# The first feed-forward's down product as seven half-size products, in a hybrid retention and attention block

## Chip, cores and metric

One core of one Trainium2 chip. The time is the device time of one execution in microseconds. A kernel's figure is the median of its runs.

## The reference

One layer on 528 tokens (16 meta tokens and 512 of the input) of width 1024, in float32: a feed-forward, a mixer, a second feed-forward and a last norm.

```python
h = h + 0.5 * swiglu(rmsnorm(h, ffn1_norm), ffn1_w_gate, ffn1_w_up, ffn1_w_down)
h = h + hybrid_mixer(rmsnorm(h, mix_norm), ...)
h = h + 0.5 * swiglu(rmsnorm(h, ffn2_norm), ffn2_w_gate, ffn2_w_up, ffn2_w_down)
y = rmsnorm(h, final_norm)

def swiglu(u, w_gate, w_up, w_down):
    return (jax.nn.silu(u @ w_gate) * (u @ w_up)) @ w_down
```

The hidden width is 2816, that is 22 feature blocks of 128. The change lies in the first line: the product with `ffn1_w_down` ("the downs").

## The kernel before

**Numbers in two parts.** TensorE multiplies in a reduced format (fp32r), so every operand is split into an upper part (a rounded copy by ScalarE) and a lower part (the rest, a subtraction by VectorE; `in_two`, lines 284 and 285). A product then takes three matmuls: upper by upper, upper by lower, lower by upper (`mm3`, line 157). A block of weights is the stationary operand, 264 tokens (half of 528) the moving one.

**The first feed-forward** (class `Sevens`, object `s1`, and the lists of steps from line 868). Feature blocks go in pairs. A pair is two halves, the gate and the up; each half is one `seven` (line 440): a 2 by 2 block product done as seven half-size products instead of eight, in four steps. Run1 has the products X and Z, run2 adds to X and starts Y, run3 adds to X again and then to Y, run4 adds the last product, T4, to X. Between these, ScalarE copies partial sums out of the PSUM banks (`copy`), and VectorE takes results out (`take`, lines 512 and 526). In run3, `take(3)` reads X between the third product and T4. VectorE also makes sums of the weights for the next half (`pre2`, `pre3`, lines 458 to 464). At the end of an up half the product of gate and up lies in a tile `u`; it is split into the hidden tiles `hh` and `hl`.

**The downs before.** `down(f0, nf, taken_by)` (line 831) multiplies the hidden tiles of `nf` feature blocks by their rows of the weights: eight steps, one for each 128 output columns, each with `nf` x 3 x 2 matmuls of 128x264. The two results of a step are added by VectorE with factor 0.5 to the residual `hT` (line 849). There are four groups: blocks 0 to 3 first, then after each three pairs the six blocks these made. In the last of three pairs (`soon`) the hidden tiles are made at once.

**Leaving the stage.** In the last group each finished column tile of `hT` goes through `leave_tokens` (line 861): multiplied by the gain and split (ScalarE `xh`, line 121; VectorE `xl`, line 122), squared by ScalarE and added to the sum of squares by GpSimd (`add_square`, lines 255 and 256), and stored to DRAM on ScalarE's queue. The mixer's first tiles (`early_step`, line 947; 24 matmuls of 128x384 for the first) need these `xh` and `xl`, all eight column tiles; behind the first one TensorE does the norm's small matmuls (`rstd_steps`, line 218), which need the full sum of squares.

**What sets the order.** `steps_through` (line 295) runs all steps of the stage as one list: at step i it issues the loads and preparations of step i+4 (`pre`), the upper split of step i+2, then the matmuls of step i with the lower split of step i+2 among them. TensorE, ScalarE and VectorE keep the order of the program here; DMA queues (SP above all) and GpSimd are ordered by the framework's planner. Work put into the list `behind` is done at the next `catch_up`, after the first step's second product.

**The second feed-forward** has the change's form already (lines 2200 and on): the downs of 16 of its 22 blocks are seven products behind all of its pairs, with operands kept in DRAM (`hx`, `wx`). There GpSimd makes the differences of the hidden tiles (line 2289), and VectorE makes the block sums of the weights during the attention (`block_sums`, line 1908).

## Time and profile before

| | |
|---|---|
| median of 3 runs | 1516.91 us (1515.62 to 1517.08) |
| the profiled execution | 1517.71 us, its span 1515.9 us |
| TensorE busy | 1505.0 us, 99% of the span, 9743 matmuls |
| VectorE busy | 1137.9 us, 75% |
| ScalarE busy | 729.4 us, 48% |
| GpSimd busy | 156.6 us, 10% |
| granted TensorE clock | 0.999 of full speed |
| HBM | 180.06 MB read, 32.78 MB written, 140 GB/s over the span |

In the rows below PE is TensorE, DVE VectorE, ACT ScalarE, POOL GpSimd and SP the engine that issues most DMAs; SPq is its queue. A row of the timeline has the start in us, the duration in us, engine, line, operation and operands (out<-in), the count, and in brackets the idle time in front of it with what ended it. L157 is line 157 of the kernel before.

### The profile page before, as it was taken

How to read it: one execution, taken by the hardware profiler on the slowest of the kernel's cores; microseconds unless marked ns; L12 is line 12 of the kernel's file. 1: busy time of each engine (PE TensorE's matmuls, PEld its weight loads, DVE VectorE, ACT ScalarE, POOL GpSimd, SP SyncE). 2: the span in 40 equal slices, each digit the busy share in tenths (PEclk: the TensorE clock that was granted, in tenths of full speed). 3: DMA queues.
4: the chain of work that ended last, by engine and by line, in shares of the span. 5: the costliest groups of instructions: out<-in, count | busy, mean ns of one | idle time of the engine just before them, and what ended most of it. 6: DMA issues, size and time to landing. Idle time of an engine off the chain costs nothing.

```text
span 1515.9 us, 24279 instructions
## 1 busy us (share of the span) xinstructions
PE 1505.0 (99%) x9743; PEld 1359.7 (90%) x9743; DVE 1137.9 (75%) x1735; ACT 729.4 (48%) x1156; POOL 156.6 (10%) x188
## 2 busy tenths in 40 slices
PE   9999999999999999999999999999999999999997
PEld 8999999999988888788888889989888889999986
DVE  4988585786786767677968676777665779999877
ACT  5655263454354444542323445555335445555565
POOL 1000000003111120000000021111002003322101
PEclk9999999999999999999999999999999999999999
DMA  5132323226544444232222476456573224445792
GB/s 169 58 120 89 114 96 112 85 97 201 202 148 168 167 148 155 87 122 86 94 86 85 111 187 178 155 168 214 173 255 108 84 83 147 152 162 174 248 330 109
DMA packets 170176, 217.03 MB, mean 143 GB/s; under 512 B 7056, under 2 KB 126504, under 8 KB 169168
## 3 DMA queue, kind: packets, MB, share of 16 engines
q1 hardware_dynamic: 156592, 180.97, 36.5%
q0 software_dynamic: 9072, 26.59, 5.9%
q10 hardware_dynamic: 4400, 7.94, 1.5%
q8 instruction: 76, 1.25, 0.3%
q14 instruction: 36, 0.29, 0.1%
HBM read 180.06 MB, written 32.78 MB: 140 GB/s over the span
## 4 chain that ended last, share of the span: by engine, by line
PE 95%; DMA 2%; issue 1%; DVE 1%; ACT 1%; POOL 0%; POOLq 0%; ACTq 0%; DVEq 0%; SPq 0%
PE psqX L157 14%; PE psd L157 8%; PE psqY L157 7%; PE psrg L157 6%; PE psro L157 4%; PE psvX L1150 4%; PE psqZ L157 3%; PE psrk L157 3%; PE psak L157 3%; PE psu L157 3%; PE psrq L157 3%; PE psmo L157 3%; PE psga L157 3%; PE psat L157 3%; PE psaq L157 3%; PE psg L157 2%
## 5 line engine op out<-in xcount | busy, mean ns | idle before, releaser
L285 DVE TENSOR_TENSOR wlo<-raw,whi 128x1024 fp32r<-128x1024 f32 (+2 forms) x193 | 212.6, 1103 | 44.9 <-ACT whi L284 44.9
L284 ACT ACTIVATE whi<-raw 128x1024 fp32r<-128x1024 f32 (+2 forms) x193 | 179.6, 931 | 121.2 <-PE psd L157 37.7
L157 PE MATMUL psqX<-th,whi 128*128 128x264 f32 (+1 forms) x432 | 123.0, 285 | 0.0
L157 PE MATMUL psqX<-tl,whi 128*128 128x264 f32 (+1 forms) x432 | 122.3, 283 | 0.0
L157 PE MATMUL psqX<-th,wlo 128*128 128x264 f32 (+1 forms) x432 | 122.2, 283 | 0.0
L117 ACT ACTIVATE whi<-raw 128x1024 fp32r<-128x1024 f32 (+1 forms) x58 | 60.3, 1043 | 88.5 <-DMA raw<-in_w_in_dram 21.6
L284 ACT ACTIVATE whi<-wsum 128x1024 fp32r<-128x1024 f32 x72 | 76.1, 1057 | 53.6 <-issue 22.9
L118 DVE TENSOR_TENSOR wlo<-raw,whi 128x1024 fp32r<-128x1024 f32 (+1 forms) x58 | 69.8, 1204 | 42.5 <-ACT whi L117 42.2
L285 DVE TENSOR_TENSOR wlo<-wsum,whi 128x1024 fp32r<-128x1024 f32 x72 | 86.9, 1215 | 2.7 <-ACT whi L284 2.7
L157 PEld LDWEIGHTS psqX<-th,whi 128*128 128x128 f32 x432 | 82.0, 190 | 0.5
L157 PEld LDWEIGHTS psqX<-tl,whi 128*128 128x128 f32 x432 | 82.0, 190 | 0.0
L157 PEld LDWEIGHTS psqX<-th,wlo 128*128 128x128 f32 x432 | 82.0, 190 | 0.0
L157 PE MATMUL psro<-vo,whi 128*128 128x512 f32 x256 | 79.3, 391 | 0.0
L157 PE MATMUL psd<-hl,whi 128*128 128x264 f32 x352 | 71.2, 284 | 0.0
L157 PE MATMUL psd<-hh,wlo 128*128 128x264 f32 x352 | 70.9, 283 | 0.0
L157 PE MATMUL psd<-hh,whi 128*128 128x264 f32 x352 | 70.6, 282 | 0.0
L256 POOL TENSOR_TENSOR ssum<-ssum,sq 128x528 f32<-128x528 f32 (+1 forms) x14 | 18.4, 1317 | 396.4 <-ACT sq L255 396.4
L157 PEld LDWEIGHTS psro<-vo,whi 128*128 128x128 f32 x256 | 48.0, 188 | 10.7 <-ACT whi L284 0.2
L157 PEld LDWEIGHTS psd<-hh,wlo 128*128 128x128 f32 x352 | 54.5, 188 | 0.0
L157 PEld LDWEIGHTS psd<-hh,whi 128*128 128x128 f32 x352 | 54.3, 188 | 0.0
L157 PEld LDWEIGHTS psd<-hl,whi 128*128 128x128 f32 x352 | 53.9, 188 | 0.0
L157 PE MATMUL psrg<-xh,whi 128*128 128x512 f32 x128 | 51.8, 405 | 0.0
(478 smaller groups left out, 4645.6 us busy)
## 6 DMA issues: line engine op xcount, KB each, us to landing
raw<-in_ffn_w_up_dram SPq DMA_DIRECT2D x22, 1024.0 KB, 5.0
raw<-in_ffn_w_gate_dram SPq DMA_DIRECT2D x21, 1024.0 KB, 5.6
raw<-in_w_in_dram SPq DMA_DIRECT2D x19, 1024.0 KB, 5.1
raw<-in_w_in_dram SPq DMA_DIRECT2D x31, 512.0 KB, 3.9
w<-in_w_in_dram SPq DMA_DIRECT2D x24, 512.0 KB, 6.3
raw<-in_ffn_w_down_dram SPq DMA_DIRECT2D x22, 512.0 KB, 5.0
raw<-in_ffn_w_down_dram SPq DMA_DIRECT2D x12, 768.0 KB, 4.4
raw<-in_w_ret_out_dram SPq DMA_DIRECT2D x8, 1024.0 KB, 4.8
```

The lines of the kernel that those rows point to most:

```text
L117: nc.scalar.activation(hi, src, AF.Copy)
L118: eng.tensor_tensor(lo, src, hi.bitcast(F32), ALU.subtract)
L157: nc.tensor.matmul(o, a[:, k, :], b[:, sl], start=first and k == 0 and i == 0, stop=last and k == nk - 1 and i == 2, skip_group_check=onto)
L256: eng.tensor_tensor(ssum[:, :n], ssum[:, :n], sq[:, :n], ALU.add)
L284: nc.scalar.activation(hi, src, AF.Copy)
L285: return lambda: nc.vector.tensor_tensor(lo, src, hi.bitcast(F32), ALU.subtract)
L1150: nc.tensor.matmul(d[bank_][t], a, b[:, k, :], start=not onto and j + k + m == 0, stop=j + k == 3 and m == 2, skip_group_check=onto)
```

## The change

The four groups become: `down(0, 4)` as before, then all nine pairs of blocks 4 to 21 in one row, then a unit for the blocks 4 to 19 of seven products X, Z, U, Q, V, Y, W with a `down(20, 2)` in front of W. In a product, each of four steps has 4 x 2 x 3 matmuls of 128x264. Its operands come from DRAM: `hx1` holds the hidden tiles' four quarters and four differences of them (made by VectorE in `spill1`, behind each pair), `wx1` four sums of quarters of the down weights (made by VectorE in `sums1`, two at a time, in `pre3` of 16 sevens; their blocks are loaded by `bring1` and stored again on SP's queue). The hidden tiles of blocks 4 to 19 are no longer split in the pair, but as operands of the unit. Left column tiles (0 to 3) are finished by the last step of W, right ones (4 to 7) by `down(20, 2)`, whose steps run in the order 4, 5, 6, 7, 0, 1, 2, 3. The first early tile multiplies tiles 4 to 7 before 0 to 3. `product1` (shortened below) is the new function of the unit.

```diff
@@ Sevens
+        extra = []
@@ pre3
                 self.sum4 = lambda: nc.vector.tensor_tensor(s[:, 3], raw[:, 4:, c1], s[:, 0], ALU.subtract)
+                if self.extra:
+                    self.extra.pop(0)()
@@ leaving the stage
-        def leave_tokens(k):
-
-            h, l = new_x(k, XO)
-            split_gain(hT[k], gains[:, 1, k : k + 1], h, l)
-            add_square(hT[k], ssum2, k == 0, sqp[0], bufs=4)
-            nc.scalar.dma_start(hd[k], hT[k][:, REAL])
+        def split_tokens(k):
+            split_gain(hT[k], gains[:, 1, k : k + 1], *new_x(k, XO))
+        def leave_tokens(k, eng=nc.gpsimd, queue=nc.scalar):
+            add_square(hT[k], late["s"], k == 4, sqp[0], bufs=4, eng=eng)
+            queue.dma_start(hd[k], hT[k][:, REAL])
...
+        def spill1(f, u):
+            k = (f - F0) // 2
+            all4 = hidp.tile([P, 2, TX], F32, tag=turn(room_tags), name="ts")[:, :, :T].rearrange("p a (b t) -> p a b t", b=2)
+            ts = [all4[:, i // 2, i % 2] for i in range(4)]
+            for t, a, b in zip(ts, (u[:, 1], u[:, 3], u[:, 3], u[:, 2]), (u[:, 0], ts[0], u[:, 1], ts[1])):
+                nc.vector.tensor_tensor(t, a, b, ALU.subtract)
+            nc.gpsimd.dma_start(hx1[0:4, :, k, :].rearrange("o p t -> p o t"), u)
+            for i in range(2):
+                nc.gpsimd.dma_start(hx1[4 + 2 * i : 6 + 2 * i, :, k, :].rearrange("o p t -> p o t"), all4[:, i])
+        def bring1(k):
+            blocks["now"] = []
+            for tag, (half, cs) in zip(("R", "R", "ssum2", "wq"), BLOCKS):
+                t = hidp.tile([P, S], F32, tag="wq", name="wq") if tag == "wq" else one_row(tag)[:, :S]
+                nc.sync.dma_start(t, wrows1[half][:, k, cs])
+                blocks["now"].append(t)
+        def sums1(k, which):
+            ts = blocks["now"]
+            for i in which:
+                to, x, y, op = BLOCK_SUMS[i]
+                nc.vector.tensor_tensor(ts[to], ts[x], ts[y], op)
+                nc.sync.dma_start(wx1[i, :, k, :], ts[to])
+            if 3 in which and k < 7:
+                bring1(k + 1)
+        s1.spill = {f: (lambda u, f=f: s1.behind.append(lambda: spill1(f, u))) for f in range(F0, F1, 2)}
+        s1.extra = [lambda k=k, w=w: sums1(k, w) for k in range(8) for w in ((0, 1), (2, 3))]
+        def product1(tag, src, which, pool_of, taken, onto=None):
...
+                def run(w, lower, j=j, d=d):
+                    if j == 0 and onto is None:
+                        streams[tag] = [unit[pool_of].tile([P, S], F32, tag="bank", name=f"ps{tag}")[:, :TH] for _ in range(4)]
+                    pss = streams[onto or tag]
+                    h, l = (d["xp"][:, i] for i in range(2))
...
+                    for c in range(4):
+                        for k in range(2):
+                            for i, (a, m) in enumerate(((w[0], h), (w[0], l), (w[1], h))):
+                                nc.tensor.matmul(pss[c], a[:, k, c * P : (c + 1) * P], m[:, k, :],
...
+                        if c == 0:
+                            lower()
+                        if last:
+                            taken(c, pss[c])
+                        if c == 1:
+                            s1.catch_up()
+                            if behind:
+                                behind.pop(0)()
+        def right_done(c):
+            if c >= 4:
+                behind.append(lambda: (split_tokens(c), leave_tokens(c)))
+            if c == 1:
+                ahead[0] = 4
+            if c in (1, 3):
+                behind.pop(0)()
+        def left_done(c, ps):
+            added1((1, 0))(c, ps)
+            split_tokens(c)
+            if c == 3:
+                for k in range(4):
+                    leave_tokens(k, nc.vector, nc.sync)
         steps = down(0, 4, keep_sums)
-        groups = (4, 10, 16)
-        for f0 in groups:
-            for f in range(f0, f0 + 6, 2):
-                steps += s1.pair_steps(f, f == f0 + 4)
-            if f0 != groups[-1]:
-                steps += down(f0, 6, keep_sums)
+        for f in range(F0, NF, 2):
+            steps += s1.pair_steps(f, False)
         n_busy = len(steps)
-        steps += down(groups[-1], 6, leave_tokens)
+        steps += product1("X", wrows1[0][:, :, C1], 0, "A", added1((0, 0)))
+        steps += product1("Z", wrows1[1][:, :, C1], 2, "B", added1((0, 0)))
+        steps += product1("U", wx1[2], 5, None, added1((1, 0)), "X")
+        steps += product1("Q", wrows1[1][:, :, C2], 7, "B", added1((0, 1)))
+        steps += product1("V", wx1[1], 6, None, added1((1, 1), (0, 1)), "X")
+        steps += product1("Y", wx1[0], 4, "B", added1((1, 1)))
+        steps += down(F1, 2, right_done, (4, 5, 6, 7, 0, 1, 2, 3), load_row)
+        steps += product1("W", wx1[3], 3, None, left_done, "Y")
@@ early_step
-                mm3(outs, w, xs, KD)
+                if i == 0:
+                    mm3(outs, [t[:, 4:] for t in w], lambda k: xs(k + 4), 4, True, False)
+                    mm3(outs, [t[:, :4] for t in w], xs, 4, False, True)
+                else:
+                    mm3(outs, w, xs, KD)
@@ running the steps
+        bring1(0)
+        pipe = steps_through(steps, ahead)
...
             wss.close()
+            unit["p"] = sqs.enter_context(pool("f1u", 1, side="right"))
             sqp.append(sqs.enter_context(pool("sq", 1, side="right")))
+            ahead[0] = 6
+            bankst.close()
+            for name in "AB":
+                unit[name] = bankst.enter_context(pool(f"f1{name}", 4, PSUM))
+            s1.banks = unit["A"]
```

`ahead` is how many steps ahead the loads are issued: 4 until the unit begins, then 6, and 4 again near its end.

## Rows read from the trace of the kernel before

**Rows 1.** The page: busy times, and the chain that ended last by engine.
```profile
PE 1505.0 (99%) x9743; PEld 1359.7 (90%) x9743; DVE 1137.9 (75%) x1735; ACT 729.4 (48%) x1156; POOL 156.6 (10%) x188
...
PE 95%; DMA 2%; issue 1%; DVE 1%; ACT 1%; POOL 0%; POOLq 0%; ACTq 0%; DVEq 0%; SPq 0%
```

**Rows 2.** The chain in order of time, 60 to 400 us (start, us, what).
```profile
62.28 23.15 PE psd L157 x192
...
146.29 34.56 PE psd L157 x288
...
371.33 4.20 PE psiq L157 x24
```

**Rows 3.** Busy us by engine in the window of one middle pair.
```profile
105.60:125.80 20.20, 20.20 (x170) 20.20 (x170) 17.68 (x25) 12.26 (x19) 0.00 (x0) 1.00 0.27 88
```

**Rows 4.** Timeline of VectorE in that pair: gate half, then up half.
```profile
107.75 1.22 DVE L285 TENSOR_TENSOR wlo<-wsum,whi 128x1024 fp32r<-128x1024 f32 x1
108.89 0.42 DVE L512 TENSOR_TENSOR g<-psqZ,p 128x264 f32<-128x264 f32 x1
109.23 0.68 DVE L458 TENSOR_TENSOR wsum<-raw 128x512 f32<-128x512 f32 x1
109.95 0.69 DVE L459 TENSOR_TENSOR wsum<-wsum,raw 128x512 f32<-128x512 f32 x1
110.55 0.68 DVE L285 TENSOR_TENSOR wlo<-raw,whi 128x512 fp32r<-128x512 f32 x1
111.16 0.69 DVE L463 TENSOR_TENSOR wsum<-raw 128x512 f32<-128x512 f32 x1
113.17 0.43 DVE L512 TENSOR_TENSOR g<-psqX,p 128x264 f32<-128x264 f32 x1 [1.33 <-PE psqX L157]
...
119.29 1.25 DVE L285 TENSOR_TENSOR hl<-g,hh 128x1056 fp32r<-128x1056 f32 x1
120.46 0.68 DVE L458 TENSOR_TENSOR wsum<-raw 128x512 f32<-128x512 f32 x1
```

**Rows 5.** Timeline of VectorE and TensorE at the first pair.
```profile
82.13 0.68 DVE L463 TENSOR_TENSOR wsum<-raw 128x512 f32<-128x512 f32 x1
...
93.50 0.42 DVE L512 TENSOR_TENSOR g<-psqX,p 128x264 f32<-128x264 f32 x1
...
93.98 0.39 PE L157 MATMUL psqX<-th,whi 128*128 128x264 f32 x1
```

**Rows 6.** Timeline of VectorE in a gate half of the second feed-forward.
```profile
1303.58 1.58 DVE L463 TENSOR_TENSOR wsum<-raw 128x512 f32<-128x512 f32 x1
1305.08 0.41 DVE L512 TENSOR_TENSOR g<-psqX,p 128x256 f32<-128x256 f32 x1
```

**Rows 7.** DMA issues (KB, us to landing); a window of the second unit.
```profile
raw<-in_ffn_w_up_dram SPq DMA_DIRECT2D x22, 1024.0 KB, 5.0
...
wq<-in_ffn_w_down_dram SPq DMA_DIRECT2D x32, 256.0 KB, 5.1
...
1440.40:1451.30 10.90, 10.90 (x49) 9.02 (x49) 7.80 (x9) 6.33 (x8) 0.00 (x0) 1.00 1.04 405
```

**Rows 8.** Timeline where the mixer's first tiles begin, by engine.
```profile
371.71 0.76 DVE L849 SCALAR_TENSOR_TENSOR hT<-psd,hT 128x264 f32<-128x264 f32 x2
...
372.50 0.74 ACT L121 ACTIVATE xh<-hT,gains 128x528 fp32r<-128x528 f32 x1 [2.32 <-DVE hT L849]
373.15 0.63 ACT L255 ACTIVATE sq<-hT 128x528 f32<-128x528 f32 x1
...
373.27 0.77 DVE L122 SCALAR_TENSOR_TENSOR xl<-hT,gains,xh 128x528 fp32r<-128x528 f32 x1 [0.80 <-ACT xh L121]
373.92 1.35 POOL L256 TENSOR_TENSOR ssum<-ssum,sq 128x528 f32<-128x528 f32 x1 [3.21 <-ACT sq L255]
374.76 1.60 DVE L285 TENSOR_TENSOR wlo<-raw,whi 128x1024 fp32r<-128x1024 f32 x1 [0.71 <-ACT whi L284]
375.37 1.24 PE L218 MATMUL psn<-ones,ssum 128*128 128x1 f32 x10
```

More of the change, by code (lines that the diff above doesn't have):

```diff
@@ L258 @@
     R = cpool.tile([P, T], F32, name="R", tag="R", bufs=2)
-    R2 = cpool.tile([P, T], F32, name="R2", tag="R", bufs=2)
+    late = {}
     ssum2 = cpool.tile([P, T], F32, name="ssum2", tag="ssum2")
@@ L271 @@
     wx = dpool.tile([4, P, 8, S], F32, name="wx")
+    hx1 = dpool.tile([8, P, 8, TH], F32, name="hx1")
+    wx1 = dpool.tile([4, P, 8, S], F32, name="wx1")
+    F0, F1 = 4, 20
+    C1, C2 = slice(0, S), slice(S, D)
+    wrows1, wrows = (w[F0 * P : F1 * P, :].rearrange("(k two p) c -> two p k c", two=2, p=P) for w in (wd1, wd2))
+    BLOCK_SUMS = ((1, 2, 1, ALU.add), (2, 0, 2, ALU.subtract), (0, 1, 0, ALU.subtract), (3, 3, 0, ALU.subtract))
+    BLOCKS = ((0, C1), (1, C2), (0, C2), (1, C1))
     def gap(p, n):
@@ new lines, in product1, with pre, upper @@
+        def product1(tag, src, which, pool_of, taken, onto=None):
+            steps, ws = [], []
+            for j in range(4):
+                d = {}
+                def pre(j=j, d=d, ws=ws):
+                    is_late = ahead[0] > 4 or "p" in unit
+                    if j % 2 == 0:
+                        t = unit["p"].tile([P, 2048], F32, tag="wr", name="raw", bufs=2) if is_late and j == 0 else \
+                            wpool.tile([P, 2048], F32, tag="raw", name="raw", bufs=2)
+                        ws.append(t.rearrange("p (k c) -> p k c", k=4))
+                    d["w"] = ws[j // 2][:, j % 2 * 2 : j % 2 * 2 + 2]
+                    nc.sync.dma_start(d["w"], src[:, 2 * j : 2 * j + 2, :])
+                    d["x"] = unit["p"].tile([P, T], F32, tag="xr", name="raw", bufs=6) if is_late else one_row(turn(raw_tags))
+                    nc.sync.dma_start(d["x"].rearrange("p (k t) -> p k t", k=2), hx1[which, :, 2 * j : 2 * j + 2, :])
+                def upper(d=d):
+                    hi, lo = (wpool.tile([P, 1024 + WPAD], F32R, tag=t, name=t, bufs=3)[:, w_at[0] :][:, : 2 * S]
+                              .rearrange("p (k c) -> p k c", k=2) for t in ("whi", "wlo"))
+                    lower_w = in_two(d["w"], hi, lo)
+                    xp = hidp.tile([P, 2, TX], F32R, tag=turn(part_tags), name="xp")[:, :, :T]
+                    lower_x = in_two(d["x"], xp[:, 0], xp[:, 1])
+                    d["xp"] = xp.rearrange("p a (k t) -> p a k t", k=2)
+                    return hi, lo, lambda: (lower_w(), lower_x())
+                def run(w, lower, j=j, d=d):
[3 more added lines that the diff above has]
+                    h, l = (d["xp"][:, i] for i in range(2))
+                    first, last = j == 0 and onto is None, j == 3
+                    for c in range(4):
+                        for k in range(2):
+                            for i, (a, m) in enumerate(((w[0], h), (w[0], l), (w[1], h))):
+                                nc.tensor.matmul(pss[c], a[:, k, c * P : (c + 1) * P], m[:, k, :],
+                                                 start=first and k == 0 and i == 0, stop=last and k == 1 and i == 2,
+                                                 skip_group_check=onto is not None)
+                        if c == 0:
[6 more added lines that the diff above has]
+                                behind.pop(0)()
+                steps.append((pre, upper, run))
+            return steps
@@ new lines, in added1, with taken @@
+        def added1(*to):
+            def taken(c, ps):
+                for half, right in to:
+                    h = hT[4 * right + c][:, (one, two)[half]]
+                    nc.vector.scalar_tensor_tensor(h, ps, 0.5, h, ALU.mult, ALU.add)
+            return taken
+        def right_done(c):
[5 more added lines that the diff above has]
+                behind.pop(0)()
@@ L911, in normed_out @@
         def normed_out(i):
-            ps, r = early_ps[i], R2[:, early[i][1]]
+            ps, r = early_ps[i], late["R"][:, early[i][1]]
             if i > 6:
@@ L1241 @@
             wss.close()
+            unit["p"] = sqs.enter_context(pool("f1u", 1, side="right"))
             sqp.append(sqs.enter_context(pool("sq", 1, side="right")))
-            for _ in range(n_dense - n_busy - 4):
+            ahead[0] = 6
[3 more added lines that the diff above has]
+            s1.banks = unit["A"]
+            for _ in range(8):
+                next(pipe)
+            late["R"] = cpool.tile([P, T], F32, name="R2", tag="R", bufs=2)
+            late["s"] = cpool.tile([P, T], F32, name="ssum2", tag="ssum2")
+            for _ in range(n_dense - n_busy - 12):
                 next(pipe)
```

37 lines of the change are left out of this document (22 added, 15 removed).

## The prediction, made before the changed kernel was run

> **What bounds the kernel now.** First the page: TensorE is busy 99% of the span and makes up 95% of the chain that ended last [rows 1], so nothing else is worth asking about until it delays TensorE. Second, the chain in order of time over the first feed-forward and the mixer's first tiles [rows 2]: each down group is one unbroken piece of matmuls, 192 in 23.15 us and 288 in 34.56 us (three such groups), 0.120 us per matmul. A group of the change's kind can therefore only win by issuing fewer matmuls, and only if the other engines follow. Third, then, the engine nearest to its limit: in a middle pair of feature blocks TensorE is busy 20.20 of 20.20 us and VectorE 17.68 [rows 3]. Fourth, VectorE's own order in that pair [rows 4], where the reader should look at starts, not durations: a 0.69 us instruction is followed 0.60 us later.
>
> The profiled execution took 1517.71 us, 0.80 above the median of the three timed runs (1516.91). I sum differences against the profiled one and apply them to the median.
>
> **Matmuls.** 16 feature blocks x 8 column tiles x 2 token halves x 3 parts are 768 matmuls of 128x264. Seven products x 4 steps x 4 column tiles x 2 blocks x 3 parts are 672, of the same shape. They change the stationary block at every matmul, as the pairs do, whose 168 take 20.2 us [rows 3], also 0.120 each. So 96 x 0.120 = **-11.5 us**. ScalarE's and VectorE's splits for the unit (per step of 24 matmuls, 2.88 us: VectorE 1.14 for 1024 columns, 107.75 to 108.89 in rows 4, and about 0.62 for 528) lie beside it.
>
> **Pairs, VectorE.** Gone is the lower half of the hidden tile, 1.17 us from start to start (119.29 to 120.46). New are four token differences of 128x264, 0.34 each by the nearest row (108.89 to 109.23), and four block sums of 128x512, 0.60 each (109.95 to 110.55). An instruction that reads its predecessor's result starts 0.12 later (109.23 to 109.95), once in each four. So 17.68 - 1.17 + 1.48 + 2.52 = 20.5 us in a pair of 20.2: VectorE has nothing left. Where it hurts is run4. Its product T4 adds to the bank that VectorE must first read in run3 (`take(3)`); between them lie 12 matmuls, 1.44 us. In a gate half VectorE now reaches that read 1.33 us early [rows 4]. The differences (1.48) and two block sums (1.20) come ahead of it: 1.35 late, plus the read's 0.43 and 0.06 to TensorE, less 1.44: a stop of 0.4 us. In the up half the two block sums stand in for the hidden tile (1.20 against 1.17) and no stop follows. Pairs 2 to 8 have both in their gate half: 7 x 0.4 = 2.8.
>
> The first pair is worse. There VectorE is already behind from the first down: it reaches the read at 93.50 without any wait, the read ends at 93.92, and T4 starts at 93.98 [rows 5]. Block sums are issued behind the pre-step at 82.13 and again in front of this read, 2.4 us in all, and no idle lies between: 2.3. So **+5.1 us**. Ends: in the second feed-forward, where VectorE is slowed by GpSimd (0.69 becomes 1.58), the read at 1305.08 also comes without a wait [rows 6], and TensorE isn't stopped; if all pairs turn out so the term is 0. The upper end comes from loads, below.
>
> **Queues and transfers.** SP gets 32 block loads, 32 block stores, the unit's loads and four of the eight token stores that ScalarE's queue had; GpSimd gets 24 operand stores. Stores on SP wait for VectorE's sums, and block loads wait for stores out of the same tiles; behind them stand the weight loads. Per pair the bytes grow from 2.1 MB (88 GB/s, rows 3) to 2.1 + 1.05 + 1.05 + 1.08 = 5.3 MB, about 255 GB/s. A weight load lands in 5.0 us and a block load in 5.1 [rows 7]; free for them are about 7 us (from the last split of the old weights, 110.55 and later by the 1.48, to the sums at 120.46) and 8 us (from a pair's last store to the next pair's sums). I cost them at nothing; the cover is 2 to 3 us, and once it is gone each us is a us of TensorE, since VectorE has no slack. In the unit, 776 KB per 2.88 us are 276 GB/s; the second feed-forward's unit moved 405 GB/s in a window with TensorE fully busy [rows 7]. Nothing there, and nothing at its entry: banks change hands under running products, as there.
>
> **The unit's end, VectorE and ScalarE.** Before, the last down column needs an add (two of 128x264, 0.76), xh on ScalarE 0.74, xl 0.77, a Square 0.63 and GpSimd's 1.35 [rows 8]; only that column is left by then, and 21 of the 24 early matmuls (0.175 each, rows 2) cover it, so the norm's matmuls start at 375.37 without a gap. After the change four left columns end in the last step of W. VectorE's order there is add, wait for xh, xl, add, ...: 0.42 + 0.04 + 0.78 + 0.70 = 1.94 us per column, four times. It also begins late: through the eight short down steps (1.44 us each) and W's first two, 17.3 us, it has 8 x 0.34 + 16 x 0.35 + 4 x (1.14 + 0.62) + 4 x 0.70 = 18.1 us of work (small splits and adds as instructions of 128x264, a W step's two splits, xl), and up to four instructions are stretched by 0.37 (1.60 against 1.22) by GpSimd's adds [rows 4, 8]. In W's last step comes the lower part of the second early block first (1.14), and ScalarE can make its upper part (about as long) only when W's third step has freed a buffer: 2.3, and 2.5 with the passing on. So the first add starts 2.5 us into that step without a backlog and some 3.4 with one, and the last xl is ready after 10.3 to 11.2. TensorE has the step (2.88) and 21 early matmuls (3.7) until 6.6: it waits 3.7 to 4.6. Then the four Squares and four adds of 128x528, now VectorE's (0.62 each, bounded by the 0.70 of xl), end 2.5 us behind the last xl, while TensorE has 0.5 us left: 2.0. Small stops before W: 0.3 to 0.9. Sum 6.0 to 7.5; I take **+6.7 us**.
>
> **Sum:** -11.5 + 5.1 + 6.7 = +0.3, so 1517.2 us.
>
> One rule of the Trainium skill bears on the pairs. The row shows that the instruction behind one of 0.69 us starts after 0.60 [rows 4]. The Trainium skill, page "VectorE: DVE Perf Modes", section "The DRAIN you can't avoid", says that the next VectorE operation does not start until the pipe is empty. By starts a pair is 20.5 us and the sum +0.3; by full durations it is 23.2 us and the sum +19.2 (rival 3). The trace speaks against it here.
>
> **Rivals.**
> 1. *VectorE keeps pace in the pairs.* The overload is only 0.3 us a pair, and rows 6 show a read without wait that stops nothing. Against it rows 5: T4 starts 0.06 behind the read. Then -11.5 + 6.0 = -5.5: 1511.4.
> 2. *Late loads set the pace (slower).* Place: the wait of the block sums or of the next weights' first sums, in front of VectorE's other work. It decides when a weight load takes over 7 us or a block load over 8, at three times today's bytes per pair. For it: 5.0 and 5.1 at far lower traffic. Against it: 405 GB/s reached. Price 1 us in each of 8 pairs: +8.3, 1525.2.
> 3. *VectorE starts nothing before the last is through.* 32 instructions in a pair (25 in the window, less one, plus eight) at 0.085 us more each: 23.2 against 20.2, 8 pairs, 24 in place of 5.1, so +19.2: 1536.1. Rows 4 deny it.
> 4. *The change saves no matmuls.* The loop bounds fix 672 against 768; only a slower matmul could eat it, and the pairs' row says 0.120. Then +11.8: 1528.7.
>
> **How the numbers follow.** A measurement of this kernel can tell about 0.2%, 3.0 us, from no change. My forecast has 0.46: within 3 us 0.36, faster by more 0.04, slower by more 0.06. Rival 1 has 0.22, of which 0.18 beyond 3 us and 0.04 within. Rival 2 has 0.28, all slower. Rivals 3 and 4 have 0.02 each, slower. Together: faster 0.22, same 0.40, slower 0.38. The forecast's own range is 1513.7 to 1518.5 (at the low end only the first pair is stopped and the end costs 6.0, -11.5 + 8.3; at the high end 5.6 and 7.5). The range of 8 in 10 takes in both neighbours: 1511 to 1526, leaving out about 0.08 below and 0.10 above.
>
> **What would show it.** Right: 96 fewer matmuls; VectorE above 97% in the middle pairs; a dent of 0.4 us in TensorE in front of T4 of each gate half and about 2 us in the first; gaps of 1 to 1.5 us between the early tile's last blocks, and 2 us before the norm's matmuls; TensorE busy otherwise. Wrong: VectorE idle on DMA in the pairs (rival 2), no dent at all (rival 1), a unit whose steps take more than 2.88 us, or a stop where the unit begins, which I put at nothing.

## The result, and the profile after

The changed kernel takes **1536.84 us** (median of 4 runs, 1536.28 to 1538.21), the kernel before, beside it on the same chip, 1516.55: a ratio of 1.0136 (95% interval 1.0118 to 1.0153). It is 20.3 us slower, outside the range of the prediction. The profiled execution took 1538.21 us, its span (from the first to the last instruction) 1536.4 against 1515.9. Ratios and their intervals are of fast runs; one of the twelve runs of v3 below, at 4646.18 us, was a slow one and is in its median but not in its ratio. The page of the changed kernel, busy time by engine [rows 1]:

```profile
PE 1504.5 (98%) x9647; PEld 1354.2 (88%) x9647; DVE 1189.7 (77%) x1826; ACT 749.1 (49%) x1188; POOL 169.9 (11%) x208
```

The 96 matmuls are gone (9743 to 9647), and yet TensorE's busy time hardly fell: the same matmuls count as busy for longer where the clock is low and right behind a stop (below, 17.97 us against 14.65 from the norm to the fifth early tile, 185.49 against 182.23 in the pairs). The chain that ended last says little here: the page could follow it back over 73% of the span only. So the first question is where in the stage the time lies. The windows of the changed kernel [rows 2], cut where TensorE goes from one piece of the stage to the next (bounds and length in us, then busy time of PE, PEld, DVE, ACT and POOL, granted clock, DMA share, GB/s): the nine pairs, one middle pair [rows 3], X, Z, U, the short down group, W, the first early tile, from the norm to the fifth early tile, and two pieces of that:

```profile
84.47:281.29 196.82, 185.49 (x1515) 182.89 (x1514) 180.68 (x276) 101.59 (x164) 17.52 (x24) 1.00 0.69 226
159.00:180.60 21.60, 20.43 (x170) 20.22 (x169) 20.87 (x32) 11.17 (x18) 2.17 (x3) 1.00 0.73 245
281.29:295.81 14.52, 11.79 (x98) 11.59 (x97) 8.15 (x9) 6.23 (x9) 0.00 (x0) 1.00 0.76 267
295.81:310.29 14.48, 13.52 (x96) 13.32 (x97) 11.66 (x16) 7.86 (x10) 0.00 (x0) 0.88 1.01 361
310.29:321.92 11.63, 11.63 (x99) 11.63 (x97) 8.65 (x13) 6.38 (x8) 0.00 (x0) 1.00 0.89 290
356.80:368.33 11.53, 11.53 (x98) 11.53 (x97) 9.09 (x22) 6.45 (x12) 0.00 (x0) 1.00 0.24 81
368.33:383.10 14.77, 12.44 (x98) 11.77 (x97) 14.62 (x17) 8.87 (x14) 4.80 (x3) 1.00 0.31 105
383.10:393.38 10.28, 6.17 (x27) 4.18 (x25) 6.90 (x12) 6.75 (x10) 0.00 (x0) 0.85 0.79 252
393.38:411.47 18.09, 17.97 (x86) 17.55 (x87) 7.55 (x11) 3.38 (x5) 2.12 (x1) 0.80 0.69 234
393.00:396.00 3.00, 2.62 (x12) 2.62 (x12) 1.75 (x4) 0.49 (x1) 0.05 (x1) 0.50 0.69 255
396.00:402.00 6.00, 6.00 (x24) 6.00 (x24) 1.00 (x1) 0.00 (x0) 2.07 (x1) 0.63 0.66 210
```

The kernel before, cut in the same places, has its nine pairs in three stretches of 60.87, 60.68 and 60.68 us, its first early tile in 4.20 [rows 2], and from the norm to the fifth early tile 14.71:

```profile
85.26:146.13 60.87, 60.87 (x507) 60.77 (x506) 52.04 (x75) 34.44 (x55) 0.00 (x0) 1.00 0.30 99
180.69:241.37 60.68, 60.68 (x507) 60.68 (x506) 48.85 (x69) 34.26 (x54) 0.00 (x0) 1.00 0.30 96
...
375.37:390.08 14.71, 14.65 (x88) 14.23 (x87) 7.47 (x11) 4.32 (x5) 2.10 (x1) 1.00 1.01 358
```

That gives the whole account, in us:

| part | predicted | measured |
|---|---|---|
| matmuls (92.9 for seven undisturbed products and the short group, 103.7 for three down groups before) | -11.5 | -10.8 |
| pairs (196.82 against 182.23) | +5.1 | +14.6 |
| entry: X and Z (29.00 against two undisturbed products, 23.25) | 0 | +5.8 |
| W (14.77 against 11.62) | +0.3 to 0.9 | +3.1 |
| first early tile (10.28 against 4.20) | +5.7 to 6.6 | +6.1 |
| norm to fifth early tile (18.09 against 14.71) | 0 | +3.4 |
| the first downs begin earlier | 0 | -0.8 |
| sum at the fifth early tile (starts 411.47 and 390.08) | +0.3 | +21.4 |

The span is 20.5 longer; the 0.9 between lies in the rest of the kernel, which no edit touches and which takes 1124.8 to 1127.5 us in the 13 profiles of this case. The waits of the changed kernel name the causes. First TensorE's in the pairs, then TensorE's behind them, then SP's and VectorE's in the pairs (us in total, times, longest):

```profile
PE psqX L157 <- DVE g L522: 8.2, 8, 1.6
PE psqX L157 <- DVE g L536: 2.5, 3, 1.2
...
PE psZ L967 <- ACT xp L291: 2.7, 1, 2.7
PE psY L967 <- DVE xp L292: 2.3, 3, 1.8
PE psn L218 <- DVE ssum L256: 2.0, 1, 2.0
...
SPq L909 <- DMA wx<-hraw: 67.5, 14, 6.8
...
DVE hraw L917 <- DMA hraw<-in_ffn_w_down_dram: 2.8, 3, 1.6
```

L522 and L536 are `take(3)` of a gate half and an up half, L917 the block sums. In the pairs TensorE waits for nothing else but 0.6 us once. Eight of the eleven stops lie in gate halves, where the prediction had put them, but three lie in up halves, where it had none. The timeline of the changed kernel shows one of each: an up half, and a gate half with TensorE's T4 [rows 4]:

```profile
147.34 1.42 DVE L917 TENSOR_TENSOR hraw<-hraw 128x512 f32<-128x512 f32 x2 [1.57 <-DMA hraw<-in_ffn_w_down_dram]
148.68 0.42 DVE L536 TENSOR_TENSOR g<-psqX,p 128x264 f32<-128x264 f32 x1
...
158.30 0.68 DVE L471 TENSOR_TENSOR wsum<-raw 128x512 f32<-128x512 f32 x1
158.90 0.68 DVE L917 TENSOR_TENSOR hraw<-hraw 128x512 f32<-128x512 f32 x1
159.62 0.69 DVE L917 TENSOR_TENSOR wq<-wq,hraw 128x512 f32<-128x512 f32 x1
160.23 0.42 DVE L522 TENSOR_TENSOR g<-psqX,p 128x264 f32<-128x264 f32 x1
...
160.71 0.39 PE L157 MATMUL psqX<-th,whi 128*128 128x264 f32 x1 [1.17 <-DVE g L522]
```

Two block sums stand in front of each of these reads. In the gate half they take 0.72 and 0.61 from start to start, 1.33 together, because the second reads what the first writes; the prediction had 1.20. T4 follows 0.05 us behind the read. In the up half the sums themselves waited 1.57 us for their blocks. The DMA issues of the pairs [rows 7] (KB each, median us to landing) show what such a block waits for:

```profile
wx<-hraw SPq DMA_DIRECT2D x22, 256.0 KB, 6.0
hraw<-in_ffn_w_down_dram SPq DMA_DIRECT2D x21, 256.0 KB, 3.3
```

The load itself lands in 3.3 us, less than the 5.1 taken; but it goes into a tile from which the sum before is still being stored, and that store takes 6.0. (Both are medians.) The weight loads land later too, in 6.6 and 7.1 us instead of 5.0.

The timeline of the changed kernel where the unit begins, in W, and at the end [rows 8]:

```profile
287.48 0.81 SPq L945 DMA_DIRECT2D raw<-wx  x2
288.34 0.43 SPq L945 DMA_DIRECT2D raw<-in_ffn_w_down_dram  x1
...
294.17 1.06 ACT L291 ACTIVATE whi<-raw 128x1024 fp32r<-128x1024 f32 x1 [7.45 <-DMA raw<-in_ffn_w_down_dram]
...
369.82 1.92 POOL L256 TENSOR_TENSOR ssum<-ssum,sq 128x528 f32<-128x528 f32 x1 [102.60 <-ACT sq L255]
...
370.46 1.84 DVE L292 TENSOR_TENSOR xp<-raw,xp 128x528 fp32r<-128x528 f32 x1
...
383.76 0.77 DVE L122 SCALAR_TENSOR_TENSOR xl<-hT,gains,xh 128x528 fp32r<-128x528 f32 x1 [0.80 <-ACT xh L121]
...
389.50 0.77 DVE L122 SCALAR_TENSOR_TENSOR xl<-hT,gains,xh 128x528 fp32r<-128x528 f32 x1 [0.80 <-ACT xh L121]
390.18 3.14 DVE L256 TENSOR_TENSOR ssum<-ssum,sq 128x528 f32<-128x528 f32 x4
```

Z's first weights are issued at 288.34 and ScalarE can begin on them 5.8 us later, when X has been through since 292.9. In front of them in SP's queue stands a load of U's summed weights (`wx`, 287.48), for which SP had waited until X's last weights were split (`wlo` L292, through at 287.46). In W a split of 0.70 us takes 1.84 beside GpSimd's add. At the end a column takes 1.91 us, 0.80 of it waiting for ScalarE, and the four sums come after all of them.

### The profile page after: what moved, and what is told of

Read it like the earlier page. It is cut to its first block, busy times and chain, and to the rows that moved or that the text cites. A ratio compares the mean times of both kernels' runs of the same rounds, so it can differ in the third digit from the quotient of the medians.

```text
span 1536.4 us, 24555 instructions
## 1 busy us (share of the span) xinstructions
PE 1504.5 (98%) x9647; PEld 1354.2 (88%) x9647; DVE 1189.7 (77%) x1826; ACT 749.1 (49%) x1188; POOL 169.9 (11%) x208
## 4 chain that ended last, share of the span: by engine, by line
PE 69%; DVE 2%; issue 1%; DMA 1%; ACT 0%; POOL 0%; POOLq 0%; ACTq 0%; DVEq 0%
PE psrg L157 6%; PE psro L157 6%; PE psqX L157 6%; PE psvX L1293 4%; PE psrk L157 3%; PE psak L157 3%; PE psrq L157 3%; PE psgate L157 3%; PE psmo L157 3%; PE psga L157 3%; PE psaq L157 3%; PE psat L157 3%; PE psqY L157 3%; PE psd L2364 2%; PE psvY L1293 2%; PE pspv L1656 2%
## 5 line engine op out<-in xcount | busy, mean ns | idle before, releaser
L292 DVE TENSOR_TENSOR wlo<-raw,whi 128x1024 fp32r<-128x1024 f32 (+2 forms) x205 | 223.9, 1093 | 62.6 <-ACT whi L291 62.4
L291 ACT ACTIVATE whi<-raw 128x1024 fp32r<-128x1024 f32 (+2 forms) x205 | 192.5, 940 | 141.1 <-PE psqZ L157 20.6
L157 PE MATMUL psqX<-th,whi 128*128 128x264 f32 (+1 forms) x432 | 124.2, 287 | 10.8 <-DVE g L522 8.2
L292 DVE TENSOR_TENSOR wlo<-wsum,whi 128x1024 fp32r<-128x1024 f32 x72 | 86.2, 1214 | 1.0 <-ACT whi L291 0.9
L157 PE MATMUL psro<-vo,wlo 128*128 128x512 f32 x128 | 50.3, 393 | 0.0
L157 PE MATMUL psrg<-xh,wlo 128*128 128x512 f32 x128 | 50.0, 390 | 0.0
L157 PE MATMUL psrg<-xl,whi 128*128 128x512 f32 x128 | 49.9, 390 | 0.0
L292 DVE TENSOR_TENSOR wlo<-w,whi 128x1024 fp32r<-128x1024 f32 x30 | 36.5, 1221 | 13.1 <-ACT whi L291 13.1
L2438 POOL TENSOR_TENSOR ts<-g 128x256 f32<-128x256 f32 x16 | 22.3, 1411 | 176.3 <-DVE g L547 95.8
L291 ACT ACTIVATE whi<-w 128x1024 fp32r<-128x1024 f32 x30 | 31.7, 1057 | 20.1 <-PE psvX L1293 10.9
L157 PE MATMUL psqY<-xh,whi 128*128 128x264 f32 (+1 forms) x144 | 40.7, 283 | 0.0
```

What stands on the lines that cost most here:

```text
L157: nc.tensor.matmul(o, a[:, k, :], b[:, sl], start=first and k == 0 and i == 0, stop=last and k == nk - 1 and i == 2, skip_group_check=onto)
L291: nc.scalar.activation(hi, src, AF.Copy)
L292: return lambda: nc.vector.tensor_tensor(lo, src, hi.bitcast(F32), ALU.subtract)
L2438: nc.gpsimd.tensor_tensor(ts[:, i], a, b, ALU.subtract)
```

## The experiments

The first eight edit the changed kernel, each with one run, profiled and timed, beside the kernel before at 1516.29 to 1516.92 us. Five profiles have the pairs as in the changed kernel: its own (196.8 us), and those of the order at the end (192.3), the entry (192.9), the clock (193.0) and W (196.0). So the pairs lose 10.1 to 14.6 us with the same instructions, and a total of one run can't tell an edit's few us from that; the windows can. Whether they differ from run to run or from kernel to kernel is open: the four totals of the changed kernel lie within 1.9 us.

**Pairs: which work of VectorE, or the loads?** Three edits, first without the differences:

```diff
...
-            for t, a, b in zip(ts, (u[:, 1], u[:, 3], u[:, 3], u[:, 2]), (u[:, 0], ts[0], u[:, 1], ts[1])):
-                nc.vector.tensor_tensor(t, a, b, ALU.subtract)
...
```

> The changed kernel without the four token differences that VectorE makes behind each pair; the same bytes go to DRAM, taken from the product of gate and up itself. So the operands of U, Q, V and Y are not the reference's. Theory (VectorE has more work in a pair than TensorE's 20.2 us): 1.5 us less work stands in front of the read of X in every gate half, the stops there (0.6 to 1.2 us) go, and the pairs' stage falls from 196.8 us to about 187; the whole to 1527. Rival (block and weight loads come late behind the stores on SP's queue): they are as late as before, the stage stays above 194 and the whole above 1534.

Measured: 1534.32 us; the pairs take 189.87. All gate-half stops but the first pair's are gone, as the theory said. What stays are the first pair (0.80 and 1.77 lost) and four stops in up halves (1.75, 0.72, 0.39 and 1.13), which the theory had not counted: it was 3 us too low for the pairs. The total, 7 above the 1527 expected, lies at the rival's 1534, but not for the rival's reason: the pairs are well below its 194, and some 3 of the 7 lie in X and Z (29.75 us against 29.00) and in the untouched rest.

```diff
-        s1.extra = [lambda k=k, w=w: sums1(k, w) for k in range(8) for w in ((0, 1), (2, 3))]
+        s1.extra = []
...
```

> The changed kernel without block sums, their loads and their stores; U, V, Y and W take unsummed quarters of the down weights, so the result is not the reference's. Both theories: no pair is stopped any more, the first included; the pairs' stage is 182 to 184 us (9 x 20.2) instead of 196.8, the whole about 1523. What stays above the kernel before's 1516.6 less 11.5 is then the price of the unit's entry, of W and of the mixer's first tiles: about 18 us.

```diff
-            if 3 in which and k < 7:
-                bring1(k + 1)
```

> The changed kernel with the block sums done eight times on blocks that are loaded once: 28 of the 32 block loads are left out, the sums and their stores stay; the summed weights are not the reference's. Theory (VectorE's work): VectorE still makes 32 sums in the pairs, so the stage falls only by the waits for loads that the trace of the changed kernel shows (some 5 us): 190 to 193 us, the whole about 1532. Rival (late loads): 183 to 185 us, the whole about 1524.

Measured: 1526.07 and 1533.43 us. The windows of the pairs, without block sums and then (the second fence) with the sums, but of blocks that are loaded only once:

```profile
84.86:267.40 182.54, 182.35 (x1515) 182.14 (x1514) 160.96 (x244) 102.51 (x164) 17.55 (x24) 1.00 0.49 159
```

```profile
84.82:276.25 191.43, 184.90 (x1515) 182.79 (x1514) 180.66 (x277) 101.69 (x164) 17.55 (x24) 1.00 0.60 195
```

The kernel without block sums is 3 above the 1523 expected, though its pairs lie in the range: X and Z take 30.60 us in it. Without block sums the differences cost 0.3 us in all. With sums that wait for no load the pairs cost 9.2, with no stop left in an up half: 2.6 in the first pair and seven of 0.72 to 0.93 in the gate halves, 5.4; some 1.2 is in single matmuls of 0.23 instead of 0.12 at T4. The rest comes with the loads: 5.4 of the 14.6 in the changed kernel's own profile, 0.9 of the 10.1 in the shortest of the five.

**Pairs: place or amount?** All four block sums of a pair go behind the read, into run4 of the gate half.

```diff
@@ pre3
-                if self.extra:
-                    self.extra.pop(0)()
@@ run4
+                if src_w is self.wg and self.extra:
+                    self.extra.pop(0)()
...
```

> The changed kernel, complete, with all four block sums of a pair made behind run4's product of the gate half instead of two in front of the read of X in each half. VectorE's work is the same. Theory (the place decides: work in front of the read stops TensorE, the total is within 2% of its time): the first pair's 2.6 us go and the gate halves' 0.7 us go, the pairs' stage is 183 to 187 us instead of 196.8, the whole 1523 to 1527. Rival (the total of VectorE's work sets the pace wherever it lies): 20.5 us a pair and the waits for loads, 189 to 192, the whole about 1530.

Measured: 1531.12 us, span 1527.6. The pairs, and the four sums in one of them, by window and timeline:

```profile
85.06:270.11 185.05, 185.05 (x1514) 183.11 (x1513) 179.72 (x276) 101.51 (x164) 17.51 (x24) 1.00 0.73 241
```

```profile
155.14 0.42 DVE L522 TENSOR_TENSOR g<-psqX,p 128x264 f32<-128x264 f32 x1
...
158.69 2.13 DVE L917 TENSOR_TENSOR hraw<-hraw 128x512 f32<-128x512 f32 x3
160.86 0.69 DVE L917 TENSOR_TENSOR wq<-wq,hraw 128x512 f32<-128x512 f32 x1
```

The same instructions, the same bytes (241 GB/s) and 179.72 us of VectorE cost 2.8 us instead of 14.6, and neither TensorE nor VectorE's sums wait; the 2.8 are 27 matmuls that start 0.1 us late, most of them T4 and the one behind it. The edit does two things at once: it moves the sums, and it gives the block loads more time (in one pair the last is issued at 163.84 and its sum comes at 179.25). Against the sums at rest, which wait for no load, the place alone is worth 6.4 (9.2 less 2.8). So the amount of VectorE's work was not the limit; it stood in front of a read. The total missed what was expected: up to the fifth early tile it is 11.4 ahead of the changed kernel, in the span only 8.8. The 2.6 between lie in the untouched rest, 1127.5 us here, the longest of the 13 profiles; and this run took 3.5 us more than its span, the other single runs 1.8 to 2.0.

**The end: order on VectorE and ScalarE.** xl of a column is issued behind the add of the next:

```diff
-            split_tokens(c)
+            hl = new_x(c, XO)
...
+            nc.scalar.activation(hl[0], hT[c], AF.Identity, scale=gain)
+            lowers.append(lambda: nc.vector.scalar_tensor_tensor(hl[1], hT[c], gain, ...))
+            if c:
+                lowers.pop(0)()
...
```

> The changed kernel, complete, with one order changed at W's end: VectorE adds column c+1 before it makes the lower half of column c, so that it does not wait for ScalarE's upper half in between. Theory (a chain add, xh, xl of 1.9 us per column sets the early tile): the last xl comes 3 us sooner, the gaps of 0.4 to 0.5 us inside the early tile go, the wait in front of the norm's matmuls stays at 1.5 to 2, and with shorter gaps the granted clock does not fall behind them: 4 to 7 us less, 1530 to 1533. Rival (the sum of squares sets it anyway, and the clock falls all the same): at most 1 to 2 us less.

Measured: 1530.82 us. From the first to the fifth early tile it takes 23.85 us, after 28.37: 4.5 less. The stops between the early tile's blocks are gone, the wait for the norm stays (2.4), and the clock still falls behind it (0.90 from the norm to the fifth early tile, 16.38 us against 14.71 before), which the theory had excluded. The pairs were 4.5 shorter too, in stops of late loads, which this edit does not touch, so the total is in the expected range partly by luck.

**The entry: is a down group behind X the cover?** The short down group goes from in front of W to behind X; the right tiles are finished by Y, and up to two pieces of work are taken from `behind` at a time (not shown).

```diff
         steps += product1("X", wrows1[0][:, :, C1], 0, "A", added1((0, 0)))
+        steps += down(F1, 2, keep_sums, load=load_row)
...
-        steps += product1("Y", wx1[0], 4, "B", added1((1, 1)))
-        steps += down(F1, 2, right_done, (4, 5, 6, 7, 0, 1, 2, 3), load_row)
+        steps += product1("Y", wx1[0], 4, "B", right_done)
```

> The changed kernel, complete, with the down of blocks 20 and 21 moved from in front of W to behind X, as the second feed-forward has it; the right columns then leave with Y. Theory of the entry (Z's loads lie where the pairs' tiles were and can start only when the last hidden tile is split, so X's 11.6 us are too short a cover): the stop of 4 us in front of Z and the half clock behind it go, about 6 us. Theory of W (VectorE has 1.1 times its time in the short down steps): the stops of 2.6 us in W shrink below 1. From X's first matmul to the early tile 95 us or less instead of 101.8; the whole 1528 to 1532, since the pairs vary by some 4 us. Rival (transfers of 270 GB/s are the limit in the unit): the wait moves to Z or U all the same, 99 us or more.

Measured: 1531.02 us; from X to the first early tile 98.88, after 101.8. Both theories missed (95 or less; less than 1 us of stops in W). The number is next to the rival's 99, but its reason, the rate of the transfers, is not shown. TensorE's waits say where the time went: the stop moved to the down group's own weights, others came at the banks that pass from that group to Z, and W kept its own:

```profile
PE psY L967 <- DVE hT L988: 1.7, 2, 1.3
PE psd L157 <- ACT whi L291: 1.4, 1, 1.4
PE psZ L967 <- DVE hT L859: 1.0, 2, 0.7
```

**The clock.** Matmuls of ones, whose results are not used, fill the waits: 45 before Z, 20 before the norm's matmuls.

```diff
+                    if tag == "Z" and j == 0:
+                        for _ in range(45):
+                            nc.tensor.matmul(pss[3][:, :P], ones_r, ones_r, start=True, stop=True)
...
```

> The changed kernel, complete, with 45 matmuls of ones (128 columns, results not used) in front of Z's first and 20 in front of the norm's, so that TensorE is at work through most of two waits. Theory (the granted clock falls to half behind these stops): the granted clock stays at 1.0 behind Z's start and the 20 matmuls there at 0.22 us each go back to 0.12, 2 us; behind the norm's matmuls 3 us; together up to 5 us less, 1532, if the fillers themselves do not outlast the waits. Rival (the slow stretches come from the operands): they stay at 0.22 and the time is the same or longer.

Measured: 1535.68 us. The windows: X and Z, the first early tile's wait, and from the norm to the fifth early tile:

```profile
277.11:305.39 28.28, 28.28 (x239) 28.28 (x238) 19.82 (x24) 14.23 (x19) 0.00 (x0) 1.00 0.90 324
...
385.00:390.00 5.00, 4.56 (x14) 4.59 (x15) 3.88 (x7) 3.81 (x6) 0.00 (x0) 0.50 0.77 239
394.05:408.81 14.76, 14.64 (x88) 14.22 (x88) 6.48 (x10) 3.27 (x4) 2.12 (x1) 1.00 0.75 254
```

Behind the norm the clock is 1.00 and the stretch takes 14.76 us, as in the kernel before (14.71), not 18.09: the 3.4 there were the clock alone. At the entry the clock stayed up, but the fillers outlasted the wait, so only 0.7 was won. At the end nothing was won. In front of the early tile TensorE stood still for 5.73 us in one piece, waiting for VectorE's last add, and the clock fell there instead:

```profile
PE psiq L157 <- DVE hT L990: 5.6, 1, 5.6
```

From W's first matmul to the fifth early tile it takes 45.38 us, in the changed kernel 43.14. The total is 1.2 less only because the pairs were 3.8 shorter in this run. Why the early tile waits for that add here, and not in the changed kernel, is open.

**W: do GpSimd's adds stretch VectorE?**

```diff
-                behind.append(lambda: (split_tokens(c), leave_tokens(c)))
+                behind.append(lambda: (split_tokens(c), leave_tokens(c, nc.vector)))
```

> The changed kernel with one edit: the square sums of the right column tiles 4 to 7, that GpSimd adds during W, are added by VectorE, so that GpSimd computes nothing beside W. In the changed kernel W takes 14.77 us instead of 11.6, with stops of 0.40 and 1.76 us behind VectorE's splits of the operands, and two of these splits take 1.8 us instead of 0.70. Theory (GpSimd's adds stretch VectorE, and that makes the stops): VectorE's splits in W take 0.70 again, it has four adds of 0.62 more, about 2.5, and about 4.4 of stretch less, so W takes 12.2 to 13.5 and the whole 1 to 3 us less than the changed kernel's 1536.8. Rival (VectorE simply has too much to do in W, whoever adds the squares): W takes 15 us or more, the whole 1537 or more.

Measured: 1536.82 us; its span, 1535.0, lies among the four of the changed kernel (1533.8 to 1536.4). W by window, and the split that took 1.84 by timeline:

```profile
367.59:381.27 13.68, 12.48 (x99) 11.80 (x97) 13.53 (x20) 8.76 (x14) 0.00 (x0) 1.00 0.36 118
```

```profile
369.73 0.70 DVE L292 TENSOR_TENSOR xp<-raw,xp 128x528 fp32r<-128x528 f32 x1
```

The splits are back at 0.70 though VectorE has three instructions more, and W is 1.1 shorter, though not within the 12.2 to 13.5 expected: the stretch was a good third of W's loss. TensorE's stops behind the splits fall from 2.3 us to 0.2, and 0.9 comes new at W's end, waiting for VectorE's last adds. That the rest of the loss is the amount of VectorE's work there is argued from its 13.53 busy us of 13.68, not tried. The total shows nothing of it, with one run and pairs that differ by more. The Trainium skill, page "GPSIMD Engine Reference", section "1. Specifications", says that GpSimd shares its SBUF interfaces with VectorE and contends with instructions of two SBUF inputs; the trace agrees (0.70 alone, 1.84 beside the add).

**Versions put together.** v2 is the edits of the order at the end, the sums in run4 and the down group behind X.

> The three repairs together (order at W's end, down behind X, block sums in run4), complete. Theory: each takes away its own loss, pairs' stage 183 to 187, unit 95, early tiles 23.9 instead of 28.4: 1536.8 - 11 - 6.5 - 4.5 = 1515, within 3 us of the kernel before. Rival (one of the losses only moves on to the next stage): above 1521.

Measured: 1522.02 us, 5.7 above the kernel before. Missed: the pairs, 185.9, are in the range, but X to the first early tile takes 98.95 as in the single edit, not the 95 counted on, and from there to the fifth early tile it is 25.2 instead of 23.9, with the norm's wait (2.4) and the low clock behind it (0.81).

v3 moves work away from where it is waited for (core of the edit to v2):

```diff
+        steps += product1("Q", ...)
+        steps += product1("U", ..., "X")
+        steps += product1("V", ..., "X")
+        steps += product1("Y", wx1[0], 4, "B", right_done)
+        steps += product1("Z", wrows1[1][:, :, C1], 2, "A", z_done)
+        steps += product1("W", wx1[3], 3, None, left_done, "Y")
...
+                    for c in (0, 1) if j == 2 else (2, 3):
+                        for jj in (2, 3):
```

> Complete. v2 (1522.0 us; block sums behind the read, the short down group behind X) with three things more. The products go X, down group, Q, U, V, Y, Z, W, with Z in X's freed banks, so that the right column tiles end before Z and their splits and square sums are spread over Z's four steps. W's last two steps go column by column, so that the left tiles end 1.45 us apart over 5.8 us instead of 0.72 apart over 2.9. Each left tile's square and sum follow its split at once, not behind all four. Theory (the stops are where work of VectorE and ScalarE stands too close in front of what TensorE needs; what is left in v2 is 2.1 us in W, about 6.3 behind it with the half clock, 2.9 around the down group, 3.7 in the pairs, against 11.5 saved): W's stops and those at the end go, the norm starts without a wait and the granted clock stays at full behind it, from the first early tile to the fifth (psiq to psik) it takes 18.9 to 20 us instead of 25.2, and the whole 1512 to 1516, a little under the kernel before. Rival (the unit's end is bound by the amount of VectorE's work, whatever its order): psiq to psik stays above 22 and the whole above 1518.

Measured: 1518.34 us, the median of 12 runs, against 1516.92 of 17 (ratio 1.0005, 0.9996 to 1.0014): the same as before. Expected was a little under; total and end are the rival's numbers (above 1518, above 22), and v4 decides against its reason. From the first to the fifth early tile 22.5 us: I had undone the better order of the end in it, and a column took VectorE 2.54 us, 0.81 of it waiting for ScalarE.

v4 changes the order, and moves the right columns' four square sums from GpSimd to VectorE (core of the edit to v3):

```diff
-            behind.append(lambda: (split_tokens(4 + c), leave_tokens(4 + c)))
+            behind.append(lambda: (split_tokens(4 + c), leave_tokens(4 + c, nc.vector)))
...
+            rests.append(rest)
+            for do in rests[:-1] if c < 3 else rests[:]:
+                do()
+                rests.pop(0)
@@ down, last step of the short group: add before lower()
+                    if early:
+                        lower()
```

> Complete. v3 (1518.3 us beside 1516.9 of the kernel before) with three edits of order alone. At the end VectorE adds the next left column before it makes the lower part and the square sum of the one before, so that it doesn't wait 0.81 us for ScalarE's upper part in each of four columns (v3: 2.54 us per column, against 1.45 by TensorE). The right columns' square sums are VectorE's, so that GpSimd stretches nothing in Z (v3: splits of 0.70 and 1.22 took 1.84 and 2.35). The last step of the short down group adds its result before, not behind, the splits of a later step, so that Q finds its banks free. Theory (what is left in v3 outside the pairs, about 1.9 us behind the norm's inputs with 0.9 of half clock and half-speed columns behind it, 2.1 in Z and W, 0.8 in front of Q, is place, not amount): a column then takes VectorE 1.65 us, psiq to psik takes 19 to 20 us instead of 22.5, Z and W together 23.3 to 24.3 instead of 25.3, and the whole 1513 to 1516, faster than before by 1 to 3 us. Rival (the work per step is the limit): Z and W stay above 25 or psiq to psik above 21.5, and the whole at 1517 or above.

Measured: **1513.01 us**, the median of 8 runs, against 1517.68 of the kernel before, of 12 (ratio 0.9971, 0.9960 to 0.9981): faster than it by 0.3%, and than the changed kernel. Its windows: the pairs, X with the down group, Z with W, the first early tile, and from the norm to the fifth:

```profile
85.28:271.34 186.06, 185.28 (x1514) 183.17 (x1513) 180.12 (x276) 101.75 (x164) 17.51 (x24) 1.00 0.72 240
271.34:296.58 25.24, 23.76 (x194) 23.28 (x193) 18.46 (x36) 11.31 (x20) 0.00 (x0) 1.00 0.81 283
...
343.84:367.58 23.74, 23.52 (x194) 23.31 (x193) 22.38 (x36) 18.12 (x26) 0.00 (x0) 1.00 0.54 175
367.58:371.76 4.18, 4.18 (x26) 4.18 (x25) 4.18 (x8) 3.81 (x6) 0.00 (x0) 1.00 0.76 249
371.76:386.35 14.59, 14.57 (x87) 14.16 (x87) 8.07 (x12) 4.34 (x6) 2.11 (x1) 1.00 0.94 323
```

The end costs nothing any more (4.18 and 14.59, before 4.20 and 14.71). The rival's reason (the work per step) is out: there is as much of it as in v3, and Z with W takes 23.74, from the first to the fifth early tile 18.77. Left are 3.8 in the pairs (186.06 against 182.23), 2.1 around the down group (25.24 against 23.16 for an undisturbed product and the short group), and 1.2 in the other products.

## Why the prediction was wrong

**Right.** The matmuls (-11.5 predicted, -10.8 by the windows: 0.121 each in the unit, not 0.120). The first pair (2.3; 2.6 lost). The place of the stops in gate halves, and the mechanism: T4 0.05 us behind the read. The wait for the norm, 2.0. The first early tile's sum too, +6.1 against 5.7 to 6.6, but partly by luck: the waits inside the tile are 2.1 us, in steps of 0.36 and 0.49 where gaps of 1 to 1.5 were announced, and the other 2.0 are slower matmuls (TensorE busy 6.17 us where the same matmuls took 4.20), a term that the sum did not have.

**"Pairs, VectorE": mis-sized, 5.1 for 14.6.** VectorE's work alone is 9.2 (sums at rest). A gate half loses 0.72 to 0.93 there, not 0.4. The term that was wrong is the 1.44 us between the read and T4. The read can't start before X's third product is through, and in the kernel before it did so at 113.17 [rows 4], while T4 came at 114.35, only 1.18 later:

```profile
114.35 0.28 PE L157 MATMUL psqX<-th,whi 128*128 128x264 f32 x1
```

With 1.18, and 1.32 instead of 1.20 for the two sums, the step's own working gives 1.47 + 0.43 + 0.05 - 1.18 = 0.77. The matmul behind T4 adds 0.1, 1.2 in all pairs. In the changed kernel four of the seven gate halves lose 1.33: three of them follow an up half that late blocks had stopped, so that VectorE entered them 0.6 later. The step took each half by itself. (The 5.6 for the pairs at the high end of the forecast's own range is not derived in it.) In the middle pair of the windows VectorE is busy 20.87 of 21.60 us.

**"Queues and transfers: I cost them at nothing": fell.** The step compared one landing, 5.1 us, with 8 us free. But a block's load uses the tile out of which the last sums are being stored, so two transfers stand in a row, 6.0 and 3.3 us, together 9.3: SP waited for a store's landing before a block load 14 times, up to 6.8 us. This is rival 2 in kind, and 0.9 to 5.4 of its 8. Its mark, VectorE idle on loads, is there in the changed kernel's profile (2.8 us, 3 times, in front of the block sums; 2.0 us, twice, in front of the next weights' first sums).

**"Nothing at its entry": fell,** +5.8. I argued from the second feed-forward's unit, whose banks change hands under running products. Banks were not the matter: Z's operands came late, and behind the stop the clock fell (0.88 over Z). The account is 2.7 and 1.0 us of stops, 1.6 in 16 matmuls of 0.22 instead of 0.12, and 0.4 left. Z's first weights were issued 7 us after X had begun, behind a load for U in SP's queue that waited for X's last split, and landed 5.7 later. Whether that order in the queue held them, or their own tile, which lies where the pairs' tiles were, was not tried, and stays open; moving the down group there shrank the stop and made others.

**"Small stops before W, 0.3 to 0.9": mis-sized,** 3.1. I took GpSimd's stretch as 0.37 per instruction from a row in which the two lay side by side for 0.51 us only [rows 8]; with 1.28 us side by side it is 1.1 (0.70 to 1.84), and 1.1 of W's loss went with GpSimd's adds. For the rest, VectorE has no room there: 13.53 of 13.68 us busy even without them.

**Not in the prediction: the clock.** A stop costs more than its wait. Behind the wait for the norm 3.4 us are lost at a clock of 0.50 and 0.63, at Z another 1.6 of the 5.8. The version with fillers shows the first by itself.

**The rivals.** Rival 1 did not happen, nor rival 4. Rival 3 gives 1536.1, almost the measured time, for a reason that the trace denies: an instruction of 0.68 at 158.30 is still followed 0.60 later, and with all instructions in place but in another order the pairs lose 2.8, not 24. The prediction quoted only half of the section of the Trainium skill ("VectorE: DVE Perf Modes", "The DRAIN you can't avoid"): it says that the next operation does not start until the pipe is empty, and also that one that is not held starts earlier. The trace agrees with the second (0.60 behind 0.68); the first does not hold for the starts here. A number that fits is no evidence for its mechanism.

## What to carry to other kernels

Another engine's work belongs behind, not in front of, the read that the busy engine waits for: the same block sums cost 9 us or more in front and 2.8 behind it. How long that read may be late is read from the trace, from its start to the matmul that needs it, and not counted in matmuls. Price a load into a used tile as the store out of it and the load in a row, and every stop of the matrix engine of some us with the slow matmuls behind it. Before such a product is called a loss, look at what ends each stop: here the same matmuls and transfers in another order, with four small sums moved from GpSimd to VectorE, turned 20.3 us lost into 4.7 won.

## What the runs showed of the hardware that I had not expected

- The granted clock fell behind two places of the changed kernel: the stop of 2.7 us in front of Z, with another of 1.0 behind it (0.88 over Z), and the first early tile, 4.20 us of work in 10.28 (0.50 from 393 to 396, the lower of its two levels, 1.2 of 2.4 GHz; 0.63 from 396 to 402, a mix of both). Behind the single stops of 0.7 to 1.8 us in the pairs it did not, with 1.00 over the whole stretch. Behind the longest stop in the pairs of any run, 1.93 us in the run without GpSimd's adds, it did (0.64 from 152 to 155). With fillers in front of the norm's matmuls it was 1.00 behind them, after 0.50 from 385 to 390.
- Beside GpSimd's add of 128x528 a VectorE split of the same size takes 1.84 us instead of 0.70, with the two side by side for 1.28 us; the add itself takes 1.92 (the two after it 1.33 and 1.55) where it took 1.35 before.
